# A decoder layer on one core: gathered rows of the last token block dealt out anew, and some low parts of weights made on GpSimd

## Chip, core and metric

One core of a Trainium2 chip runs the whole kernel. The metric is the device time of one execution in microseconds. The engines are TensorE (PE, its weight loads PEld), VectorE (DVE), ScalarE (ACT), GpSimd (POOL) and SyncE (SP), which only issues DMAs here.

## The reference

One layer of a decoder on 512 tokens of width 1024: a combined projection into 16 SSD heads and 8 latent-attention heads, one output projection, layer norms, and then a PEER mixer. Only the last part matters for the change. For each token, eight heads choose 16 of 16384 experts each; expert e adds its gate times gelu(u_e . x) times v_e:

```python
u = jnp.take(u_table, expert_idx, axis=0)
act = jax.nn.gelu(jnp.einsum('td,thkd->thk', xb, u).astype(jnp.float32), approximate=False)
v = jnp.take(v_table, expert_idx, axis=0)
return jnp.einsum('thk,thkd->td', (gate * act).astype(xb.dtype), v)
```

All of it is float32, and the tables hold 16384 rows of 1024 each.

## The kernel before

TensorE multiplies float32 numbers as a high and a low part. `Stream` (L93 to L140) brings each weight tile of 128x1024 (0.524 MB) in three steps: a load into a raw buffer `wir`, issued on SP's queue (L104, three raw buffers); the high part `wih` (or `wihx`, for every fourth item) by ScalarE, L122; and the low part `wil` = raw minus high, L132, by the engine that `self.lo(n)` names for item n. Before the change this is the engine in `lo_on[0]`: GpSimd during one earlier phase, VectorE in the rest. The low part of an item is made two items before TensorE uses it, and there are three buffers of it.

The mixer runs in two ways at once. For the first 384 tokens (three blocks) TensorE goes through the whole tables. The activations of a U chunk (128 experts) take 24 matmuls with 320 moving columns, three for each of eight slices (L85 to L87; the last 64 of the 384 tokens are not among these columns, their U products were made from gathered rows earlier). A V chunk takes 18 matmuls with 512 columns (L1671, L1672, L1675). Before a V chunk, its activations are multiplied with the gates `gt` into `P` (VectorE, L1631, and ScalarE, L1634 and L1635), and `P` is split into `Ph` (ScalarE, L1654) and `Pl` (VectorE, L1662). The gates of four V chunks come in one tile `gt` of 128x12x4x32 numbers (SP's queue, L1598). There are 128 U chunks; 88 are done when the V loop begins. The V loop first runs 14 V chunks alone (V0 to V13, GAP), then 40 pairs of one U and one V chunk (V14 to V53), then V alone to the end (V54 to V127). The last seven V chunks are held and run after the loop.

For the last block of 128 tokens nothing goes through TensorE. `gather()` (L1522 to L1572) fetches, for slot s = 0 to 127, one row of the u table for each token with an indirect DMA (issued by GpSimd, L1538), and VectorE multiplies and sums it (L1553); then, for s = 128 to 255, one row of the v table for each token, added to `ac` by VectorE (L1559). There are five row buffers: the gather of row s+4 is issued ahead of the work on row s and waits for the work on row s-1. After row 255 comes the layer norm of `ac` and its store.

All instructions of an engine run in the order in which the program writes them. In the loop over V chunks (L1711 on) a block for chunk c writes, for VectorE: `Pl` of chunk c+1, `P` of c+2, the low part for two items later (inside `item()`), and then as many rows of `gather()` as `dots_to()` asks for. How many that is comes from `units()`: a pair counts 2, a V chunk alone counts WV, ENDU units at the end are left free, and `dots_to` keeps the row count in proportion to the units that are gone. While rows remain with fewer than ENDU units left, the loop pulls the rest faster.

Of the kernel before, what the change touches and what calls it, by code (L numbers as in the profile page):

```python
# [40 lines left out]
PRE = 88  # L41
AHEAD = 76
GAP = max(0, PRE - LEAD - 1)
# [4 lines left out]
T_Q = 6.3  # L48
ROWS = 5
GP = 4  # L50
ENDU = 11
WV = 0.86
GST = (1, 3, 5, 7)
LOWA = (*range(2, 32, 2), 34, 38)
SCB = 6
# [11 lines left out]
def tile_block(ctx: ExitStack, tc: tile.TileContext, I, out):  # L67
    nc = tc.nc
    ctx.enter_context(tc.manual_schedule())
    V, A, T, G = nc.vector, nc.scalar, nc.tensor, nc.gpsimd  # L70
# [185 lines left out]
    items = []  # L256
    plan = items.extend
    lo_on = [V]
# [14 lines left out]
    win = Stream(wst, "wi", items, [128, 1024], raw=3, la=2, lo=lambda n: lo_on[0])  # L273
# [1042 lines left out]
    def pump(g, us):  # L1316
        bal[0] = min(bal[0] + us, us)
        while bal[0] > 0:
            c = next(g, None)
            if c is None:  # L1320
                bal[0] = 0.0
                return False
            bal[0] -= c
        return True
# [332 lines left out]
    def v_lo():  # L1657
        if pend:
            c, P, Ph = pend.pop()
            Pl = v_sb(c, "Pl")  # L1660
            for (t, a, b), (h, _, _) in zip(Pl, Ph):
                V.tensor_tensor(t, P[:, a:b], h, op=OP.subtract)  # L1662
            blk = lambda z: [t[:, i:i + 128] for t, a, b in z for i in range(0, b - a, 128)]
            PP[c] = (blk(Ph), blk(Pl))
# [25 lines left out]
    for c in range(2):  # L1690
# [5 lines left out]
        v_hi(c, v_prep(c))  # L1696
        v_lo()
    more = True
    units = lambda: (128 - uc) * 2 + WV * (uc - vc)
    fin = None  # L1700

    def dots_to():
        if not GS[1]:
            GS[1:] = units() - ENDU, GS[0]
        want = 253 - max(0.0, (256 - GS[2]) * (units() - ENDU) / GS[1])
        more = True
        while more and GS[0] < want:
            more = pump(fill, 0.1)
        return more

    while vc <= LASTC:  # L1711
# [16 lines left out]
        else:  # L1728
            more = more and dots_to()
            if more and units() < ENDU:  # L1730
                more = pump(fill, 1.8)
# [149 lines left out]
```

## Time and profile before

| | us |
|---|---|
| median of 3 runs | 1551.11 |
| lowest, highest | 1545.24, 1552.41 |
| profiled execution, its own time | 1547.06 |
| span of the profiled execution | 1545.0 |
| TensorE busy | 1523.8 |
| VectorE busy | 1353.2 |
| GpSimd busy | 646.7 |

The last block's work runs beside the V loop, from about 865 us to 1490 us of the span. A timeline row gives the start and the duration in microseconds; instructions of one engine overlap a little at their ends, so the cost of one is better read from start to start. Where like instructions follow each other the row gives their number and the duration from the first start to the last end. A gap in front is given in brackets with what ended it.

### The profile page before, as it was taken

To read this page: it belongs to the slowest core of one execution; us is meant where nothing else is said; L and a number is where in the kernel's file an instruction comes from. 1 tells how busy PE (TensorE), PEld (TensorE's weight loads), DVE (VectorE), ACT (ScalarE), POOL (GpSimd) and SP (SyncE) were. 2 spreads that over 40 slices of the span, in tenths; PEclk is the share of its full clock that TensorE was granted. 3 is DMA by queue.
4 is the path that set the end of the run, shared out by engine and by line. 5 is a ranking of instruction groups with operands and counts; after the bars stand their busy time and mean duration, and the time that the engine had idled before them with its cause. 6 is when DMAs were issued, how large, how long until landed. Compare 5 with 4: busy or idle time off the path is not lost.

```text
span 1545.0 us, 24621 instructions
## 1 busy us (share of the span) xinstructions
PE 1523.8 (99%) x8696; PEld 1338.0 (87%) x8696; DVE 1353.2 (88%) x2609; ACT 760.9 (49%) x1415; POOL 646.7 (42%) x469
## 2 busy tenths in 40 slices
PE   9999999999999999999999999999999999999997
PEld 7787888888888999999999889999988888888886
DVE  8979767656799999999998689998989999999997
ACT  5574477742433454667666544444433444444442
POOL 0000032420244522435430566666656767767610
PEclk9999999999999999999999999999999999999999
DMA  6242122374422566999998999999999999999983
GB/s 258 96 148 99 57 71 59 109 249 162 140 76 90 148 210 216 347 340 357 375 337 290 375 401 389 382 369 392 378 362 387 398 389 383 390 375 389 372 299 148
DMA packets 153595, 417.52 MB, mean 270 GB/s; under 512 B 15472, under 2 KB 56704, under 8 KB 153216
## 3 DMA queue, kind: packets, MB, share of 16 engines
q1 hardware_dynamic: 95712, 210.28, 39.3%
q0 software_dynamic: 52352, 187.25, 32.4%
q10 hardware_dynamic: 5408, 18.43, 3.0%
q8 instruction: 68, 1.11, 0.3%
q14 instruction: 55, 0.45, 0.1%
HBM read 383.52 MB, written 30.21 MB: 268 GB/s over the span
## 4 chain that ended last, share of the span: by engine, by line
PE 70%; DMA 10%; DVE 7%; issue 6%; POOL 4%; ACT 2%; DVEq 0%; POOLq 0%; ACTq 0%
PE pu L85 7%; PE va L1672 7%; PE va L1675 7%; PE va L1671 7%; PE pu L87 7%; PE pu L86 7%; DMA row<-u,ix 6%; POOL row L1538 4%; PE pw L85 3%; PE pw L87 3%; PE pw L86 3%; PE pa L86 3%; PE pa L87 3%; PE pa L85 3%; DMA wir<-ut 2%
## 5 line engine op out<-in xcount | busy, mean ns | idle before, releaser
L122 ACT ACTIVATE wih<-wir 128x1024 fp32r<-128x1024 f32 (+2 forms) x269 | 277.7, 1034 | 238.0 <-DMA wir<-ut 137.6
L132 DVE TENSOR_TENSOR wil<-wir,wih 128x1024 fp32r<-128x1024 f32 (+1 forms) x232 | 280.2, 1209 | 65.5 <-ACT wih L122 51.5
L87 PE MATMUL pu<-XT,wil 128*128 128x320 f32 x1000 | 309.3, 309 | 1.7 <-DVE wil L132 1.6
L1672 PE MATMUL va<-wil,Ph 128*128 128x512 f32 x726 | 283.5, 391 | 2.4 <-DVE wil L132 2.3
L1538 POOL DMA_INDIRECT row<-v,ix x128 | 220.8, 1725 | 98.5 <-DVE ac L1559 79.7
L85 PE MATMUL pu<-XT,wih 128*128 128x320 f32 x824 | 257.6, 313 | 0.5 <-ACT aout L1413 0.5
L86 PE MATMUL pu<-XT,wih 128*128 128x320 f32 x824 | 254.5, 309 | 0.0
L1538 POOL DMA_INDIRECT row<-u,ix x128 | 181.6, 1419 | 137.4 <-DVE row L1553 73.3
L87 PEld LDWEIGHTS pu<-XT,wil 128*128 128x128 f32 x1000 | 187.7, 188 | 2.5 <-DVE wil L132 2.5
L1671 PE MATMUL va<-wih,Ph 128*128 128x512 f32 x486 | 189.2, 389 | 0.0
L1559 DVE SCALAR_TENSOR_TENSOR ac<-row,hd,ac 128x1024 f32<-128x1024 f32 x128 | 164.0, 1281 | 3.1 <-DMA row<-v,ix 1.5
L1672 PEld LDWEIGHTS va<-wil,Ph 128*128 128x128 f32 x726 | 136.3, 188 | 31.2 <-DVE wil L132 4.0
L1553 DVE SCALAR_TENSOR_TENSOR row<-row,XT 128x1024 f32<-128x1024 f32 x128 | 153.4, 1220 | 11.1 <-DMA row<-u,ix 10.9
L85 PEld LDWEIGHTS pu<-XT,wih 128*128 128x128 f32 x824 | 154.7, 188 | 2.6 <-ACT aout L1413 0.7
L1132 POOL DMA_INDIRECT urow<-u,uix x64 | 98.3, 1536 | 138.3 <-DVE urow L1138 119.2
L86 PEld LDWEIGHTS pu<-XT,wih 128*128 128x128 f32 x824 | 154.8, 188 | 1.5
L1675 PE MATMUL va<-wih,Pl 128*128 128x512 f32 x486 | 149.8, 390 | 0.3 <-DVE Pl L1662 0.3
L132 POOL TENSOR_TENSOR wil<-wir,wih 128x1024 fp32r<-128x1024 f32 (+3 forms) x37 | 77.7, 2107 | 146.9 <-ACT wih L122 110.8
L1654 ACT ACTIVATE Ph<-P 128x384 fp32r<-128x384 f32 x121 | 62.7, 518 | 119.6 <-DVE P L1631 108.7
L1675 PEld LDWEIGHTS va<-wih,Pl 128*128 128x128 f32 x486 | 91.1, 188 | 19.8 <-DVE Pl L1662 0.9
L1671 PEld LDWEIGHTS va<-wih,Ph 128*128 128x128 f32 x486 | 91.2, 188 | 18.2
L122 ACT ACTIVATE wihx<-wir 128x1024 fp32r<-128x1024 f32 x67 | 70.9, 1058 | 68.3 <-DMA wir<-v 49.6
(508 smaller groups left out, 3343.7 us busy)
## 6 DMA issues: line engine op xcount, KB each, us to landing
wir<-ut SPq DMA_DIRECT2D x128, 512.0 KB, 6.5
wir<-v SPq DMA_DIRECT2D x128, 512.0 KB, 7.1
gt<-gsp SPq DMA_DIRECT2D x63, 256.0 KB, 9.1
wir<-wo SPq DMA_DIRECT2D x26, 512.0 KB, 4.2
gsp<-stg ACTq DMA_DIRECT2D x21, 448.0 KB, 6.8
wir<-wf SPq DMA_DIRECT2D x18, 512.0 KB, 3.4
wir<-wqr SPq DMA_DIRECT2D x16, 512.0 KB, 3.7
asp<-aout SPq DMA_DIRECT2D x35, 160.0 KB, 5.6
```

Source lines behind the costliest of these rows:

```text
L85: T.matmul(ps, lh, rh, start=start, stop=False)
L86: T.matmul(ps, lh, rl, start=False, stop=False)
L87: T.matmul(ps, ll, rh, start=False, stop=stop)
L122: A.activation(h, r, AF.Copy)
L132: self.lo(n).tensor_tensor(l, r, h, op=OP.subtract)
L1132: G.indirect_dma_start(out=UR[n], out_offset=None, in_=I["u"], in_offset=bass.IndirectOffsetOnAxis(ap=UR["ix"][:, n:n + 1], axis=0))
L1538: G.indirect_dma_start(out=R[s], out_offset=None, in_=I["u"] if s < 128 else I["v"], in_offset=bass.IndirectOffsetOnAxis(ap=ix3[:, s % 128 ...
L1553: V.scalar_tensor_tensor(wide(r), wide(r), 1.0, x3, op0=OP.mult, op1=OP.mult, accum_out=hd[:, s:s + 1])
L1559: V.scalar_tensor_tensor(ac, r, hd[:, s - 128:s - 127], ac, op0=OP.mult, op1=OP.add)
L1671: T.matmul(va[b][e], Ph[b], h[:, cs], start=c == 0, stop=False)
L1672: T.matmul(va[b][e], Ph[b], l[:, cs], start=False, stop=False)
L1675: T.matmul(va[b][e], Pl[b], h[:, cs], start=False, stop=c == 127)
```

## The change

Two constants of the row dealing change: a V chunk alone counts 1.0 units instead of 0.86, and 13 units at the end are left free instead of 11. And in the V loop the low part of the weight tile of V chunks 56, 60, 64, ... 112 is made by GpSimd instead of VectorE. `win` is the stream of weight tiles, `items` the list of its tiles (the last 74 are V54 to V127), and `G` is GpSimd.

```diff
-ENDU = 11
-WV = 0.86
+ENDU = 13
+WV = 1.0
...
     more = True
+    first = 128 - PRE + GAP
+    relief = range(len(items) - 128 + first + 2, len(items) - 128 + 113, 4)
+    win.lo = lambda n: G if n in relief else lo_on[0]
     units = lambda: (128 - uc) * 2 + WV * (uc - vc)
```

With PRE = 88 and GAP = 14, `first` is 54.

## Rows read from the trace of the kernel before

**Rows 1.** The page's first part: busy time, share of the span, instructions.

```profile
PE 1523.8 (99%) x8696; PEld 1338.0 (87%) x8696; DVE 1353.2 (88%) x2609; ACT 760.9 (49%) x1415; POOL 646.7 (42%) x469
```

**Rows 2.** Stretches: length, busy us (instructions) by engine, clock, DMA share, GB/s.

```profile
core 0: us, PE busy (x) PEld busy (x) DVE busy (x) ACT busy (x) POOL busy (x), PEclk, DMA share, GB/s
922.00:1090.00 168.00, 168.00 (x928) 152.00 (x928) 152.90 (x231) 73.53 (x130) 109.75 (x77) 1.00 1.00 382
1090.00:1238.00 148.00, 143.69 (x776) 127.27 (x776) 134.54 (x172) 56.48 (x98) 92.86 (x66) 1.00 1.01 383
1238.00:1500.00 262.00, 261.83 (x1155) 216.36 (x1154) 254.11 (x308) 111.99 (x199) 167.34 (x94) 1.00 1.02 373
```

**Rows 3.** The same for L85 alone, a third of a U chunk's matmuls.

```profile
922.00:1090.00 168.00, 54.58 (x177) 33.08 (x178) 1.00 1.00 382
1090.00:1238.00 148.00, 44.21 (x143) 26.84 (x143) 1.00 1.01 383
```

**Rows 4.** Waits in 1090 to 1238 us: total us, times, longest.

```profile
DVE row L1553 <- DMA row<-u,ix: 5.2, 9, 1.3
DVE wil L132 <- ACT wih L122: 4.5, 2, 3.1
...
PE va L1672 <- DVE wil L132: 2.3, 3, 1.0
...
PE pu L87 <- DVE wil L132: 1.6, 2, 0.9
```

**Rows 5.** Timeline of VectorE in the V-alone stretch: start, duration, instruction.

```profile
1300.29 1.28 DVE L1559 SCALAR_TENSOR_TENSOR ac<-row,hd,ac 128x1024 f32<-128x1024 f32 x1
1301.48 0.55 DVE L1662 TENSOR_TENSOR Pl<-P,Ph 128x384 fp32r<-128x384 f32 x1
1301.95 0.48 DVE L1631 TENSOR_TENSOR P<-act,gt 128x320 f32<-128x320 f32 x1
1302.35 1.22 DVE L132 TENSOR_TENSOR wil<-wir,wih 128x1024 fp32r<-128x1024 f32 x1
1303.49 2.60 DVE L1559 SCALAR_TENSOR_TENSOR ac<-row,hd,ac 128x1024 f32<-128x1024 f32 x2
1306.00 0.55 DVE L1662 TENSOR_TENSOR Pl<-P,Ph 128x384 fp32r<-128x384 f32 x1
```

**Rows 6.** Timelines of GpSimd and VectorE where GpSimd makes low parts.

```profile
400.43 4.79 POOL L132 TENSOR_TENSOR wil<-wir,wih 128x1024 fp32r<-128x1024 f32 x2 [81.20 <-ACT wih L122]
...
401.29 1.28 DVE L198 BATCH_NORM_STATS2 lmst<-xm 128x6 f32<-128x512 f32 x2
...
403.41 1.82 DVE L188 SCALAR_TENSOR_TENSOR lma<-lmy,lmh 128x1 f32<-128x1 f32 x1
...
405.46 0.22 DVE L188 SCALAR_TENSOR_TENSOR lma<-lmy,lmh 128x1 f32<-128x1 f32 x1
...
230.89 1.29 POOL L132 TENSOR_TENSOR wil<-wir,wih 128x512 fp32r<-128x512 f32 x1 [5.05 <-PE pt L815]
...
230.93 1.26 DVE L562 TENSOR_TENSOR gv<-ssq 128x4 f32<-128x4 f32 x1
```

**Rows 7.** Timeline of GpSimd in the V-alone stretch: the gathers.

```profile
1299.48 1.70 POOL L1538 DMA_INDIRECT row<-v,ix  x1 [0.30 <-DVE P L1631]
1301.83 2.55 POOL L1538 DMA_INDIRECT row<-v,ix  x1 [0.65 <-DVE ac L1559]
1305.03 1.87 POOL L1538 DMA_INDIRECT row<-v,ix  x1 [0.65 <-DVE ac L1559]
```

**Rows 8.** Waits in 1238 to 1500 us.

```profile
ACT Ph L1654 <- DVE P L1631: 106.4, 55, 4.0
...
DVE wil L132 <- issue: 2.8, 6, 0.8
```

**Rows 9.** Waits of SP's queue in 1238 to 1500 us.

```profile
SPq L104 <- DVE wil L132: 206.6, 65, 4.5
```

**Rows 10.** DMA issues in 1238 to 1500 us: times, KB, median us to landing.

```profile
wir<-v SPq DMA_DIRECT2D x65, 512.0 KB, 7.1
...
row<-v,ix POOLq DMA_INDIRECT x92, 8.0
```

## The prediction

> **What bounds the kernel now.** I read the page's busy line first [rows 1]: TensorE is busy 99% of the span, so a change can only win where TensorE waits, or lose by making it wait. So I cut the last block into stretches [rows 2] and compared each with TensorE's own pace. In the V-alone stretch, 1238 to 1500 us, 1155 matmuls fill 262 us: 0.2268 us each, 18 per V chunk, so 4.08 us a chunk. In 922 to 1090 us, 177 x 3 = 531 of the 928 matmuls belong to U [rows 2, 3]; the other 397 take 90.0 us at the V pace, which leaves 78.0/531 = 0.147 us per U matmul, 3.53 us per U chunk and 7.6 us per pair of a U and a V chunk. By these two prices the 776 matmuls of 1090 to 1238 us (about 430 U, 346 V) need 141.7 us, and the stretch is 148: some 6.3 us are lost there, at the end of the U chunks, and nothing that I can see in the others. TensorE's recorded idle time in the stretch is 148.00 - 143.69 = 4.3 us [rows 2]. So what the redistribution can give back lies between 4.3 and 6.3 us: 0.3 to 0.4% of the time, below the 0.5% that a measurement of this kernel can tell from no change.
>
> What ends those waits is VectorE's low part of a weight, L132 [rows 4]; VectorE itself had waited there for gathered rows (5.2 us) and for high parts (4.5 us), while the DMA engines were fully used (share 1.01 at 383 GB/s, [rows 2]).
>
> V-alone has no loss but little room: VectorE is busy 254.11 of 262 us [rows 2]. Its order in a chunk is in [rows 5]: Pl, P, low part, then one or two rows. From start to start Pl takes 0.47, P 0.40, the low part 1.14 us; one row 1.19 us, two rows 2.51. A chunk with one row is 3.20 us of VectorE, with two 4.52.
>
> **The change, part by part.**
>
> *Rows dealt out.* `dots_to` gives 256 rows over `units()-ENDU` counted from the first chunk (uc = 88, vc = 1). Before: 80 + 0.86 x 87 - 11 = 143.8 units, so a pair (2 units) gets 3.56 rows and a V-alone chunk (0.86) 1.531. After: 80 + 87 - 13 = 154, so a pair gets 3.325 and a V-alone chunk 1.662. Both end at vc = 116 (0.86 x 12 = 10.3 is under 11, 12 under 13), so the tail moves only with what TensorE loses before it. 40 pairs give up 9.4 rows; 13 early V chunks take 1.7 of them, the late ones 8.
>
> In the pairs this removes 0.235 rows a pair from VectorE (about 0.28 us), and of the DMA load as much: (2 weights + 3.56 rows) x 0.524 MB plus 0.197 MB of gates is 3.11 MB per 7.6 us, 409 GB/s wanted; 392 afterwards. The stretch of 922 to 1090 us ran at 382 without loss, 1090 to 1238 got 383 with loss [rows 2]. I take it that nearly all of the loss goes: gain 4.3 to 6.3, taken at 6, since 392 is nearer to the demand that cost nothing.
>
> In V-alone VectorE's chunk goes from 3.20 + 0.531 x 1.32 = 3.90 to 3.20 + 0.662 x 1.32 = 4.07 us against TensorE's 4.08. By itself that still fits, and costs nothing only because the low part leaves on every fourth chunk, if it does leave; else there is no cover left.
>
> *The low parts on GpSimd.* `relief` names V chunks 56, 60, ... 112: 15 of them (the last 74 items are V54 to V127, so the index points where it should). Each takes 1.14 us from VectorE and puts on GpSimd the same subtraction, 2.40 us (two in 4.79, [rows 6]). Whether that is 2.40 us beside VectorE or 2.40 us in its place decides everything, and V-alone shows no such operation. The nearest rows are earlier in the same trace [rows 6]. While two of these subtractions ran (400.43 to 405.22 us), a VectorE operation on 128x1 with two inputs in SBUF, L188, took 1.82 us and ended at 405.23; the same line takes 0.22 us right behind. At 230.93 us a 128x4 operation, L562, took 1.26 us and ended within 0.01 us of GpSimd's (230.89 + 1.29). BATCH_NORM_STATS2, with one input, ran beside the first pair at its usual pace (401.29, two in 1.28). So a two-input operation stands still until GpSimd is through. All of VectorE's V-alone operations (Pl, P, low part, row) have two inputs in SBUF [rows 5].
>
> The other way round is seen at the gathers [rows 7]: the one from 1299.48 ends at 1301.18, 0.89 us after VectorE's step from low part to row at 1300.29; that from 1301.83 at 1304.38, 0.89 after the step at 1303.49; that from 1305.03 at 1306.90, 0.90 after 1306.00. GpSimd waits for the end of a VectorE instruction and then gets in, though VectorE is never idle. So I expect the subtraction to get in at such a step as well, and VectorE to stand for its length.
>
> The Trainium skill says so outright ("SBUF — State Buffer", section "SBUF: two separate sides"): the port pair that VectorE and GpSimd share is an exclusive lock, kept for the whole instruction, and a VectorE operation with two SBUF inputs contends for it with a GpSimd operation that reads SBUF. It speaks against this change, and the trace agrees (1.82 us where 0.22 is usual); by it a relief costs VectorE the difference of 2.40 and 1.14 us, without it each would save 1.14.
>
> Price: VectorE stands 2.2 us (1024 columns at (2.40 - 1.29)/512 us) to 2.40 us, so each relief costs it 1.06 to 1.26 us net, 15 of them 15.9 to 18.9; I take 17.4.
>
> The sum for V-alone, blocks 54 to 110 (57 of them, all 15 reliefs): VectorE 57 x 4.07 = 232.2 + 17.4 = 249.6 us. Add its waits: in V-alone now 262 - 254.1 = 7.9 us, of which 2.8 are its own lead (waits for a buffer of a low part, [rows 8]); bounds 0 and 5, taken 2. TensorE 57 x 4.08 = 232.6. Against this stands VectorE's lead when V-alone begins: at most 5.4 us (a chunk of 4.08, since a low part needs the buffer that TensorE frees a chunk earlier, and 1.3 as Pl is needed after four matmuls, 0.9 us into a chunk, and takes 0.5), at least 0; taken 2.7. TensorE's new waiting is 249.6 + 2.0 - 232.6 - 2.7 = 16.3 us; bounds 232.2 + 15.9 - 232.6 - 5.4 = 10.1 and 232.2 + 18.9 + 5 - 232.6 = 23.5.
>
> *What stands behind the moved instruction.* On GpSimd: the next gather. A row has five gather pitches of 13.1 us in all, less 1.2 for its own operation; a gather of up to 2.55 us and a landing of 8.0 [rows 7, 10] leave 1.3. The subtraction holds GpSimd for 2.4 us plus up to 1.3 for VectorE's running instruction, but VectorE stands for 2.4 of it: 0 to 1.3 us a relief. I take 0, since no row was late in V-alone (the rest is a rival). On SP: the load of the item three later waits for the raw buffer, now released by GpSimd (VectorE's release is what SP's queue waits for today, 206.6 us in 65 waits, [rows 9]), up to 2.5 us later; landing takes 7.1 us [rows 10] where two chunks are 8.2, so ScalarE's high part may be 1.4 us late. That is covered by ScalarE's waits for P, 106.4 us in 55 [rows 8], some 1.9 us each; without that cover it would come on top, 1.4 x 15 = 21 us at most.
>
> **Sum.** -6 + 16.3 = +10.3 us, with ends +3.8 (10.1 - 6.3) and +19.2 (23.5 - 4.3). The profiled execution took 1547.06 us (span 1545.0), 4 us under the median of the three runs, 1551.11; the middle of these four is 1549.1, and I put the sum on that: 1559, ends 1553 and 1568.
>
> **Rivals.**
> *GpSimd's low parts run beside VectorE.* Then V-alone needs 232.2 - 15 x 1.14 = 215 us of VectorE against 232.6, TensorE never waits, and only the gain in the pairs is left: 1549.1 - 4.3 to 6.3, about 1544, within 0.5%. For it: VectorE's one-input operations do run beside GpSimd. Against it: the two held operations of [rows 6].
> *The gathers behind the subtraction come too late.* 15 x 1.3 = 19.5 us on top: 1578. It decides once a relief delays a gather by more than the 1.3 us of slack; against it, VectorE stands still meanwhile.
> *The pairs don't recover*, because the late weight loads and not the rows hold them (4.5 us of waits for high parts against 5.2 for rows, [rows 4]): no gain, 16.3 us lost, 1565.
>
> **Chances.** Forecast 0.70, low parts beside VectorE 0.20, late gathers 0.05, no recovery 0.05. Of the forecast's width (+3.8 to +19.2) two thirds lie above +7.7 us, which is 0.5%: slower 0.46 + 0.10 = 0.56, same 0.24 + 0.16 = 0.40, faster 0.04 (the first rival with a little more than I count). The range of 8 in 10 takes the forecast's ends and half of the first rival: 1543 to 1568.
>
> **What would show it.** Right: 15 GpSimd rows of L132 with 2.4 to 3.7 us in V-alone; a VectorE operation beside each that takes 2 us more than its kind; TensorE waiting for Pl (L1662) or low parts between 1238 and 1500 us, with some 208 matmuls per 50 us instead of 222 (222 x 232.6/248.9); the stretch before it some 6 us shorter, without waits. Wrong: VectorE operations of usual length beside those 15, and no fewer matmuls per 50 us; then the time falls by some 5 us. If VectorE waits for rows in V-alone, it is the gathers.

## The result and the profile after

The changed kernel took 1564.18 us (median of 6 runs, 1559.39 to 1565.63), the kernel before 1548.31 beside it; the ratio is 1.0102, with a 95% interval of 1.0082 to 1.0121. It is 1% slower, some 16 us. The profiled execution took 1563.25 us, with a span of 1561.5.

The stretches of the profile after answer to [rows 2] (length; busy us and instructions of PE, PEld, DVE, ACT, POOL; clock; DMA share; GB/s):

```profile
922.00:1090.00 168.00, 168.00 (x927) 151.96 (x926) 150.83 (x227) 75.89 (x134) 99.14 (x75) 1.00 1.00 381
1090.00:1238.00 148.00, 148.00 (x805) 133.10 (x804) 137.55 (x179) 61.16 (x104) 94.43 (x65) 1.00 1.02 387
1238.00:1520.00 282.00, 271.43 (x1159) 215.92 (x1159) 275.74 (x297) 106.69 (x196) 199.70 (x113) 0.99 0.99 352
```

The pairs' stretch, 1090 to 1238 us, is full now: 805 matmuls where there were 776, and no idle time of TensorE. V-alone is slower: 1159 matmuls take 282 us, where 1155 took 262 before.

Because the time up to the V loop differs a little from execution to execution, the readings below go by stages of the V loop. They are taken from the first and last starts of three lines; of the profile after these are (count, duration min/median/max in ns, first and last start):

```profile
L1671 PE MATMUL va<-wih,Ph x486: 387/389/628, 866.1 to 1520.2; 128*128 128x512 f32 x162
...
L85 PE MATMUL pu<-XT,wih x824: 302/309/413, 516.9 to 1223.5; 128*128 128x320 f32 x165
...
L1675 PE MATMUL va<-wih,Pl x486: 389/389/727, 867.0 to 1520.9; 128*128 128x512 f32 x162
L1675 PE MATMUL va<-wihx,act x6: 388/389/389, 1535.9 to 1552.5; 128*128 128x512 f32 x6
```

The V loop's first matmul starts at 866.1, the last U chunk at 1223.5, the loop's last Pl matmul at 1520.9, the last matmul of the seven held chunks at 1552.5. So the early V chunks with the pairs took 357.4 us, V-alone 297.4, the held chunks 31.6, and 9.0 are left behind them. All profiled kernels (the experiments are told below), in us:

| kernel | up to the V loop | early V and pairs | V-alone | held chunks | rest | span |
|---|---|---|---|---|---|---|
| before | 864.9 | 363.4 | 278.8 | 28.9 | 9.0 | 1545.0 |
| after | 866.1 | 357.4 | 297.4 | 31.6 | 9.0 | 1561.5 |
| deal_only | 869.9 | 357.4 | 281.7 | 31.3 | 9.8 | 1550.1 |
| relief_only | 867.3 | 358.1 | 287.7 | 31.8 | 8.9 | 1553.8 |
| relief_8th | 867.5 | 357.4 | 286.2 | 32.3 | 8.9 | 1552.3 |
| extra_sub | 866.6 | 361.2 | 306.6 | 32.2 | 8.9 | 1575.5 |
| extra_copy | 865.5 | 358.6 | 297.5 | 34.7 | 8.7 | 1565.0 |
| extra_fill | 866.6 | 362.9 | 279.1 | 29.7 | 8.9 | 1547.2 |
| deal_half | 867.3 | 357.4 | 278.0 | 33.9 | 8.7 | 1545.3 |
| deal_early | 864.6 | 359.5 | 277.6 | 29.9 | 9.0 | 1540.6 |

At TensorE's pace (0.2268 and 0.147 us a matmul) the column of early V and pairs comes to about 357 and that of V-alone to about 277.6; the lowest measured are 357.4 and 277.6, called the floors below. The change gave 6.0 us in the pairs and lost 18.6 in V-alone and 2.7 in the held chunks; 1.2 us lie ahead of the V loop: -6.0 + 18.6 + 2.7 + 1.2 = 16.5, the difference of the spans.

What became of VectorE in V-alone is plain in the timeline after, GpSimd first (start, duration, instruction):

```profile
1298.28 1.86 POOL L1538 DMA_INDIRECT row<-v,ix  x1 [0.65 <-DVE ac L1559]
1300.16 2.40 POOL L132 TENSOR_TENSOR wil<-wir,wih 128x1024 fp32r<-128x1024 f32 x1
...
1316.00 2.60 POOL L132 TENSOR_TENSOR wil<-wir,wih 128x1024 fp32r<-128x1024 f32 x1
```

```profile
1299.25 0.55 DVE L1662 TENSOR_TENSOR Pl<-P,Ph 128x384 fp32r<-128x384 f32 x1
1299.72 3.20 DVE L1631 TENSOR_TENSOR P<-act,gt 128x320 f32<-128x320 f32 x1
1302.85 1.27 DVE L1559 SCALAR_TENSOR_TENSOR ac<-row,hd,ac 128x1024 f32<-128x1024 f32 x1
...
1316.28 2.74 DVE L1662 TENSOR_TENSOR Pl<-P,Ph 128x384 fp32r<-128x384 f32 x1
1318.94 0.48 DVE L1631 TENSOR_TENSOR P<-acts,gt 128x320 f32<-128x320 f32 x1
```

P, 0.48 us in [rows 5], takes 3.20; Pl, 0.55, takes 2.74. From start to start P costs 3.13 instead of 0.40 us, Pl 2.66 instead of 0.47. The 15 reliefs hit P nine times (2.96 to 3.14 us), Pl twice and a row three times (4.67 to 4.79 for two rows instead of 2.51); beside one of them VectorE was waiting for gates anyway. Together VectorE stood for 24.4 + 4.4 + 6.6 = 35.4 us, and was spared 15 x 1.14 = 17.1.

TensorE then waits for VectorE's Pl. In V-alone before (1238 to 1500 us) that came to 0.2 us for its matmuls and 0.8 for its weight loads. Waits in 1232 to 1520 us after (total, times, longest):

```profile
PEld va L1675 <- DVE Pl L1662: 17.2, 22, 1.6
...
PE va L1675 <- DVE Pl L1662: 7.6, 9, 1.2
...
DVE ac L1559 <- DMA row<-v,ix: 0.5, 1, 0.5
```

The third row answers one rival: VectorE waited once, for 0.5 us, for a gathered row. Nor did the loads behind GpSimd's low parts hurt. SP's queue waited for the raw buffer of a relief 4.2 us each, against 3.4 for one of VectorE's (1225 to 1520 us; compare [rows 9]), and ScalarE waited 1.8 us in all for V weights (`wir<-v`) between 1232 and 1520 us:

```profile
SPq L104 <- DVE wil L132: 172.3, 51, 4.6
SPq L104 <- POOL wil L132: 63.2, 15, 4.9
```

### The profile page after: what moved, and what is told of

The parts are those of the page before. It is cut to its first block, busy times and chain, and to the rows that moved or that the text cites. A ratio compares the mean times of both kernels' runs of the same rounds, so it can differ in the third digit from the quotient of the medians.

```text
span 1561.5 us, 24647 instructions
## 1 busy us (share of the span) xinstructions
PE 1530.7 (98%) x8696; PEld 1336.5 (86%) x8696; DVE 1370.9 (88%) x2594; ACT 758.3 (49%) x1415; POOL 670.8 (43%) x484
## 4 chain that ended last, share of the span: by engine, by line
PE 74%; DVE 11%; DMA 7%; issue 5%; ACT 3%; POOL 0%; DVEq 0%; SPq 0%; ACTq 0%; POOLq 0%
PE pu L85 9%; PE pu L87 9%; PE pu L86 9%; PE va L1675 7%; PE va L1672 7%; PE va L1671 6%; PE pw L85 3%; PE pw L87 3%; PE pw L86 3%; PE pa L87 3%; PE pa L86 3%; PE pa L85 3%; DMA row<-v,ix 2%; DMA wir<-v 2%; DMA wir<-ut 2%
## 5 line engine op out<-in xcount | busy, mean ns | idle before, releaser
L132 DVE TENSOR_TENSOR wil<-wir,wih 128x1024 fp32r<-128x1024 f32 (+1 forms) x217 | 262.2, 1209 | 69.1 <-ACT wih L122 45.5
L85 PE MATMUL pu<-XT,wih 128*128 128x320 f32 x824 | 257.6, 313 | 0.8 <-ACT aout L1413 0.7
L1538 POOL DMA_INDIRECT row<-v,ix x128 | 210.5, 1645 | 81.6 <-DVE ac L1559 58.0
L1538 POOL DMA_INDIRECT row<-u,ix x128 | 177.2, 1385 | 144.5 <-DVE row L1553 83.1
L132 POOL TENSOR_TENSOR wil<-wir,wih 128x1024 fp32r<-128x1024 f32 (+3 forms) x52 | 116.4, 2243 | 151.3 <-ACT wih L122 113.7
L1559 DVE SCALAR_TENSOR_TENSOR ac<-row,hd,ac 128x1024 f32<-128x1024 f32 x128 | 170.6, 1333 | 2.5 <-DMA row<-v,ix 0.8
L85 PEld LDWEIGHTS pu<-XT,wih 128*128 128x128 f32 x824 | 154.7, 188 | 3.0 <-ACT aout L1413 1.3
L1675 PEld LDWEIGHTS va<-wih,Pl 128*128 128x128 f32 x486 | 90.1, 189 | 32.2 <-DVE Pl L1662 14.3
```

The lines of the kernel that those rows point to most:

```text
L85: T.matmul(ps, lh, rh, start=start, stop=False)
L132: self.lo(n).tensor_tensor(l, r, h, op=OP.subtract)
L1538: G.indirect_dma_start(out=R[s], out_offset=None, in_=I["u"] if s < 128 else I["v"], in_offset=bass.IndirectOffsetOnAxis(ap=ix3[:, s % 128 ...
L1559: V.scalar_tensor_tensor(ac, r, hd[:, s - 128:s - 127], ac, op0=OP.mult, op1=OP.add)
L1675: T.matmul(va[b][e], Pl[b], h[:, cs], start=False, stop=c == 127)
```

## The experiments

The theory was the lock: while GpSimd reads SBUF, VectorE operations with two SBUF inputs stand still. The rivals were density (more rows per V-alone chunk cost the time by themselves) and the queue (gathers come late behind the moved instruction). Two runs take the change apart, three put an extra GpSimd instruction into the kernel before, one changes the dose, two look for a better dealing. The runs of before beside the new dealing, the reliefs alone, the subtraction and the fill had a median of 1546.92 us, those beside the other four 1546.29.

**New dealing alone.**

```diff
-ENDU = 11
-WV = 0.86
+ENDU = 13
+WV = 1.0
```

> The kernel before with the new dealing of rows alone (ENDU 13, WV 1.0); VectorE makes all low parts from U88 on. If GpSimd's low parts stop VectorE (lock): the pairs lose their waits (-6 us) and V-alone just fits (57 x 4.07 = 232.2 us of VectorE, some 2 us of waits, against 232.6 of TensorE and up to 5.4 us of lead), so 4 to 6 us faster than before, some 1543, without TensorE waits in V-alone. If the denser rows themselves cost V-alone its time (density): most of the 18.6 us that V-alone lost stays, so 5 to 12 us slower than before.

1550.28 us (12 runs, 1543.16 to 1556.17), ratio 1.0017 with 1.0001 to 1.0033. The lock's expectation (4 to 6 us faster) missed by 7 us and more, and the 5 to 12 us of density were not reached. The table shows where: the pairs are at their floor (357.4), but V-alone takes 281.7 us (4.1 over its floor) and the held chunks 31.3 instead of 28.9. A further 5.0 us of this execution lie ahead of the V loop, where both kernels run the same instructions, so one profile doesn't place the 3.4 us between the medians. The one wait of TensorE's matmuls in V-alone stands behind a late gate tile; VectorE, then TensorE:

```profile
1418.21 0.49 DVE L1631 TENSOR_TENSOR P<-acts,gt 128x320 f32<-128x320 f32 x1 [2.86 <-DMA gt<-gsp]
```

```profile
1422.88 1.22 PE L1675 MATMUL va<-wih,Pl 128*128 128x512 f32 x2 [2.02 <-DVE Pl L1662]
1423.90 0.63 PE L1671 MATMUL va<-wih,Ph 128*128 128x512 f32 x1
1424.33 0.63 PE L1672 MATMUL va<-wil,Ph 128*128 128x512 f32 x1
```

The wait is 2.0 of the 4.1 us. Behind it TensorE's granted clock was 0.50, the level of 1.2 GHz, from 1423 to 1426 us: the eight matmuls from 1422.88 to 1426.29 took 3.41 us, 1.6 more than at 0.2268 each.

Such waits for gates are in the kernel before too (the longest 1.5 us), but there VectorE needs 3.90 us a chunk against TensorE's 4.08, and TensorE's matmuls waited only 0.2 us for Pl. With 4.07 us of work per 4.08 it has no lead, and a late tile goes through to TensorE. That the lead makes the difference is argued here; the dealing half way, below, bears on it.

**Reliefs alone**, rows dealt as before.

```diff
+    first = 128 - PRE + GAP
+    relief = range(len(items) - 128 + first + 2, len(items) - 128 + 113, 4)
+    win.lo = lambda n: G if n in relief else lo_on[0]
```

> The kernel before, rows dealt as before, with GpSimd making the 15 low parts. Lock: each relief costs VectorE about 2.36 us and saves 1.14, 15 x 1.22 = 18 us on 57 x 3.90 = 222.3 us, plus 2 us of waits, against 232.6 us of TensorE and no lead (the pairs end with TensorE waiting as before): about 10 us slower than before (7 to 13), all of it in V-alone, the pairs' 6 us lost as before. Density: no change from before. Late gathers behind the subtraction: VectorE waits for rows in V-alone.

1559.63 us (4 runs), 12.7 more than before; ratio 1.0090 with 1.0075 to 1.0104. V-alone takes 287.7 us, 10 over its floor. The profiled execution (1555.61) is 4.0 us under the median: its span is only 8.8 us over that of before, with V-alone 8.9 longer, the held chunks 2.9, the part ahead of the V loop 2.4, and the pairs 5.3 shorter though dealt as before. So the reliefs are most of the change's loss: 0.90% of 1.02%, with 0.17% from the new dealing. Density alone is out.

**Fewer reliefs.** The changed kernel with every eighth V chunk relieved.

```diff
-    relief = range(len(items) - 128 + first + 2, len(items) - 128 + 113, 4)
+    relief = range(len(items) - 128 + first + 2, len(items) - 128 + 113, 8)
```

> The changed kernel with a relief at every eighth V chunk (8 instead of 15). Lock: 7 reliefs fewer give back 7 x 1.22 = 8.5 us of V-alone's loss: 8 us faster than the changed kernel, some 8 us slower than before. If reliefs were worth their place and the density cost the time: slower than the changed kernel, since VectorE is spared less.

1554.63 us (10 runs), ratio 1.0058 with 1.0039 to 1.0078: between the new dealing alone and the change, as the lock has it. The V-alone stage is 11.2 us shorter than with 15 reliefs; 8.5 were expected.

**One subtraction more on GpSimd.** `also` is called behind each low part; `dummy` names the same 15 places as `relief`.

```diff
                 self.lo(n).tensor_tensor(l, r, h, op=OP.subtract)
+                self.also(n, r, h)
...
+    xs3 = [XT[:, i:i + 2].rearrange("p a b -> p (a b)") for i in (10, 12, 14)]
+    win.also = lambda n, r, h: G.tensor_tensor(xs3[2], xs3[0].bitcast(F32), xs3[1].bitcast(F32), op=OP.subtract) if n in dummy else None
```

> The kernel before, with VectorE making all its low parts, and at the same 15 places GpSimd makes one more subtraction of 128x1024 whose result is not used; its inputs and its result lie in a part of XT that is free by then. Lock: VectorE stands 2.2 to 2.7 us each time and is spared nothing: 222.3 + 15 x 2.36 + 2 - 232.6 = 27 us slower than before (22 to 32). Queue (what costs is only that GpSimd's queue and the gathers behind are held): VectorE operations of usual length beside the subtraction, waits for rows, no more than the 10 us of the reliefs alone.

1577.61 us (4 runs), 30.7 more than before, ratio 1.0204 with 1.0186 to 1.0221. VectorE is spared nothing and stands as in the change, 36.5 us in all from start to start (seven times at P, four at Pl, four at a row), so the loss is more than twice that of the reliefs. The group of the extra instruction (busy, mean ns, idle before it), one of the held VectorE instructions, and TensorE's waits in 1220 to 1500 us:

```profile
L1704 POOL TENSOR_TENSOR XT<-XT 128x1024 fp32r<-128x1024 f32 x15 | 45.8, 3055 | 0.3
```

```profile
1328.27 2.75 DVE L1664 TENSOR_TENSOR Pl<-P,Ph 128x384 fp32r<-128x384 f32 x1
```

```profile
PE va L1677 <- DVE Pl L1664: 13.2, 18, 1.4
```

(In this kernel and the next two the lines behind L95 stand one to two lines lower.)

**A fill instead.** GpSimd only writes.

```diff
+    scr = XT[:, 12:16].rearrange("p a b -> p (a b)").bitcast(F32)
+    win.also = lambda n, r, h: G.memset(scr, 0.0) if n in dummy else None
```

> As the run with the extra subtraction, but the extra GpSimd instruction only writes (a fill of 128x2048 in the free part of XT), meant to hold GpSimd's queue about as long. Lock against GpSimd operations that read SBUF: within 4 us of before, VectorE operations of usual length beside it. Lock against any GpSimd operation that uses SBUF: slower by 15 times its length less some 8 us. Queue: as slow as with the extra subtraction, in proportion to its length, with VectorE waiting for rows.

1546.04 us (10 runs), ratio 0.9998 with 0.9987 to 1.0009: nothing lost. The fill holds GpSimd's queue for 1.83 us, and VectorE goes on beside it (the fill at 1302.35, VectorE's operations from 1302.65):

```profile
L1704 POOL MEMSET XT<- 128x2048 f32 x15 | 27.5, 1831 | 0.0
```

```profile
1302.65 0.55 DVE L1664 TENSOR_TENSOR Pl<-P,Ph 128x384 fp32r<-128x384 f32 x1
1303.28 0.49 DVE L1633 TENSOR_TENSOR P<-act,gt 128x320 f32<-128x320 f32 x1
1303.69 1.22 DVE L133 TENSOR_TENSOR wil<-wir,wih 128x1024 fp32r<-128x1024 f32 x1
```

Pl's step is 0.63 instead of 0.47 us here. Beside all 15 fills VectorE's instructions keep their lengths, within 0.05 us, and in V-alone VectorE waited once, for 0.2 us, for a gathered row. The gathers behind a fill are late by its length just as well, so holding GpSimd's queue for 1.8 us costs nothing, and the queue rival falls at that length.

**A copy instead**: one input in SBUF, the size of the fill.

```diff
+    xc = [XT[:, i:i + 4].rearrange("p a b -> p (a b)") for i in (8, 12)]
+    win.also = lambda n, r, h: G.tensor_copy(xc[1], xc[0].bitcast(F32)) if n in dummy else None
```

> As the run with the extra fill, but GpSimd copies 128x2048 within the free part of XT: one input in SBUF where the fill had none, the same size. Lock against GpSimd operations that read SBUF: VectorE operations stand for its length (some 1.8 us), 15 x 1.8 = 27, less some 10 us of room in V-alone: 15 to 22 us slower than before. Lock against operations with two inputs alone: as before, like the fill.

1567.14 us (one run), 20.8 more than before. The copy takes 2.16 us against the fill's 1.83, but VectorE stands beside it, 29 us in all 15 places (the copy, then Pl):

```profile
1303.05 2.13 POOL L1704 CAST XT<-XT 128x2048 fp32r<-128x2048 f32 x1
```

```profile
1303.34 2.25 DVE L1664 TENSOR_TENSOR Pl<-P,Ph 128x384 fp32r<-128x384 f32 x1
```

So it is the reading that stops VectorE, not the queue and not the writing; one input is enough. The time rests on one run, the standing on 15 places in its trace.

**Rows dealt half way**, no reliefs.

```diff
-ENDU = 11
-WV = 0.86
+ENDU = 12
+WV = 0.93
```

> Rows dealt half way (WV 0.93, ENDU 12: 3.44 rows a pair, 1.60 a V-alone chunk), no reliefs. VectorE's V-alone chunk is 3.20 + 0.60 x 1.32 = 3.99 us against 4.08, so it builds up a lead of 0.09 us a chunk. If what the new dealing alone loses in V-alone and at its end comes from VectorE having no lead there: 0 to 4 us faster than before. If it comes from the denser transfers: about half of the loss stays, within 2 us of before.

Ratio 0.9979 with 0.9963 to 0.9995 (12 runs, median 1545.13): a little faster than the kernel before, some 3 us by the ratio and 1.2 by the medians. That alone doesn't exclude the denser transfers (within 2 us of before). The trace speaks for the lead: VectorE waited for gates no less than with the new dealing alone (5.8 us in five waits against 4.5 in four, 1232 to 1500 us), yet TensorE's matmuls didn't wait there. Pairs (357.4) and V-alone (278.0) are at their floors; with 0.09 us of slack a chunk, V-alone carries the late tiles.

**Rows given to the early V chunks.**

```diff
-    units = lambda: (128 - uc) * 2 + WV * (uc - vc)
+    units = lambda: (128 - uc) * 1.9 + WV * (uc - vc) + 0.25 * max(0, GAP - vc)
```

> Rows taken from the pairs (3.40 instead of 3.56) and given to the first 13 V chunks (1.99 instead of 1.53), V-alone at the end as before (1.54), no reliefs. If the pairs' waits come from the rows beside U chunks: 2 to 5 us faster than before, V-alone and its end as before. If the early chunks can't take them (the DMA engines are full there too, 400 GB/s): TensorE waits before 922 us and nothing is won.

Ratio 0.9985 with 0.9968 to 1.0001 (median 1544.20): not told apart from before with certainty. The early chunks lose 1.2 us (55.85 of 57 us busy, where before had 57.00), as the second expectation has it; the pairs have no idle time (148.00 us busy in 1090 to 1238), as the first has it. V-alone is at its floor:

```profile
865.00:922.00 57.00, 55.85 (x244) 45.21 (x243) 45.23 (x67) 26.51 (x55) 40.83 (x44) 1.00 1.02 393
...
1238.00:1500.00 262.00, 262.00 (x1158) 216.94 (x1157) 251.31 (x305) 108.44 (x198) 147.31 (x91) 1.00 1.01 366
```

## Why the prediction was right, step by step

The direction, the mechanism and the time held (1559 forecast, 1564 measured, 1543 to 1568 given). The size was too small: 10.3 us more were forecast and 15.9 measured between the medians. In the spans it is 16.5: V-alone lost 18.6 instead of 16.3, the held chunks 2.7 and the part ahead of the V loop 1.2 where nothing was put down.

- **The price of a relief.** 17.4 us for 15 were forecast, from a hold of 2.2 to 2.4 us read off three GpSimd subtractions elsewhere in the trace [rows 6]; the trace after gives 35.4 - 17.1 = 18.3. The hold is 2.16 to 2.73 us: beside P it is longer than the bound, since VectorE's wait begins up to 0.45 us ahead of GpSimd's own row (1299.72 against 1300.16 above). The rule that the Trainium skill states ("SBUF — State Buffer", section "SBUF: two separate sides"), an exclusive lock that counts for two-input VectorE operations only against GpSimd operations that read SBUF, is borne out in both its parts: subtraction and copy cost 30.7 and 20.8 us, the fill of the copy's size nothing.
- **GpSimd gets in between VectorE's instructions**, read off the gathers [rows 7]: right, but not always at the next step. All 15 subtractions were through within 3.5 us; the two longest rows (3.49 us from 1262.82, 3.50 from 1369.23) let Pl and P pass at their usual steps (0.47 and 0.40) and held the row behind them. In the run with the extra subtraction four let Pl, P and a low part pass, and their rows are 4.6 us long. What decides it isn't shown.
- **V-alone's balance.** 16.3 us of new waiting forecast over TensorE's pace; V-alone took 18.6 more than before, 19.8 over its floor. Of the 3.5 that are missing 0.9 is the price and 2.5 VectorE's waits: 4.0 for one gate tile and 0.5 for a row, where 2.0 were taken. The reliefs alone cost V-alone 10 us over its floor, where the expectation was about 10.
- **The tail.** "The tail moves only with what TensorE loses before it": wrong by 2.7 us. The held chunks took 31.6 us instead of 28.9; TensorE stood 2.1 us for a high part whose load came late:

```profile
1532.77 1.06 ACT L122 ACTIVATE wihx<-wir 128x1024 fp32r<-128x1024 f32 x1 [2.61 <-DMA wir<-v]
```

```profile
1534.34 0.50 PE L1671 MATMUL va<-wihx,act 128*128 128x512 f32 x1 [2.09 <-ACT act L1654]
```

  ScalarE reaches P and Ph of the last chunk only behind that high part. The stage varies from 28.9 to 34.7 us in the table, also without reliefs (33.9 in deal_half), so it isn't the change's alone. Its 126 matmuls need 28.6 us at 0.2268; what is added is mostly this wait for the last chunk's high part of P (none listed in before, 0.2 us in extra_fill, up to 2.9 in extra_copy), and behind it, in deal_half and extra_copy, a granted clock of 0.50 for some 3 and 7 us. What makes the load late wasn't tried.
- **The gain of the dealing.** The term of 6 us is right for this pair of profiles (363.4 to 357.4), but too large in general: the stage, with the same instructions in it, took 363.4, 358.1, 361.2, 358.6 and 362.9 us in the kernels that deal as before, 360.8 in the mean, so what there is to win is 3.4 us on average, not 6.
- **The dealing in V-alone.** "By itself that still fits" was too hopeful, though the prediction adds that without the reliefs there is no cover left. It fits in the mean, 4.07 against 4.08, but without a lead a late tile can become lost time, and the new dealing alone ended 0.17% slower than before, not 0.3% faster. The forecast held these waits (2.0 us) but added them to the reliefs only.
- **The rivals.** Low parts beside VectorE, at 0.20, fell by the timeline; late gathers by a single wait of 0.5 us; the pairs did recover. What the prediction says for the first rival, that VectorE's one-input operations run beside GpSimd, holds for BATCH_NORM_STATS2 and not for all of them (below).
- **The chances.** Of the forecast's width (+3.8 to +19.2) 11.5 of 15.4 us lie above +7.7: three quarters, not two thirds. By its own terms slower should have had 0.62 and same 0.34.

## What to carry to other kernels

As far as these runs show, work moved from VectorE to GpSimd is spared only if it doesn't read SBUF, or if VectorE's operations beside it are of a kind that goes on (those with two SBUF inputs don't); else VectorE stands for GpSimd's whole, slower instruction, and the move costs the difference (here 2.4 for 1.1 us each). Look for two rows that settle this in the trace you have: a small VectorE operation that took as long as the GpSimd one beside it. And when work is dealt between two stages, leave the fuller one a few per cent: at 4.07 of 4.08 us V-alone lost 4.1 us over its floor, at 3.99 it lost 0.4 (one profile each), and the ratios to before (1.0001 to 1.0033 against 0.9963 to 0.9995) don't overlap.

## What the runs showed of the hardware beyond that

- A GpSimd copy with one SBUF input stops a two-input VectorE operation as a two-input subtraction does: Pl took 2.25 us beside a copy of 2.13, where 0.55 is usual.
- A GpSimd fill of 128x2048 (1.83 us) leaves VectorE's two-input operations at their length (0.55, 0.49, 1.22 us); in the place shown only the step from Pl to P grew, by 0.16 us.
- Not every one-input operation of VectorE goes on either. In the kernel before, beside the low parts that GpSimd makes in an earlier phase, a scaling of 128x384 took 2.18 us, where the same line takes 0.29 for 128 columns and 0.35 for 256 with GpSimd idle (GpSimd's subtractions run from 309.45 us on, three of them to 316.86); BATCH_NORM_STATS2 [rows 6] did not. Which of them stand wasn't tried. VectorE's timeline:

```profile
309.25 0.54 DVE L737 TENSOR_TENSOR thl<-pt,thh 128x384 fp32r<-128x384 f32 x1
...
309.89 2.18 DVE L836 TENSOR_SCALAR P<-P,sm 128x384 f32<-128x384 f32 x1
311.99 0.41 DVE L737 TENSOR_TENSOR thl<-pt,thh 128x256 fp32r<-128x256 f32 x1
```

  The subtraction thl at 311.99 us, with one of its two inputs in PSUM (`pt`), kept its length beside GpSimd's run: 0.41 us for 256 columns, where 0.54 for 384 ran mostly ahead of it.
- VectorE's wait can begin ahead of the GpSimd instruction's own row: P stood from 1299.72 us, with the subtraction's row from 1300.16 to 1302.56 right behind a gather. The nine waits of P out of the 14 were of this kind, eight of them by some 0.45 us and one by 0.27. GpSimd's rows in a profile are rough, so whether GpSimd held VectorE that early or its row starts late isn't shown.
- TensorE's granted clock can fall behind a wait. In deal_only, after a wait of 2.0 us, it was 0.50 (the level of 1.2 GHz) from 1423 to 1426 us, and matmuls followed each other in 0.43 us instead of 0.23; in the change it was 0.50 from 1432 to 1434 us, behind waits of 0.7 and 1.1. Behind the 2.1 us in the held chunks of the change, and 2.7 in those of extra_sub, it stayed at 1.00. What decides it isn't shown.
